# Result tiles of an output projection that start as loads and take products straight from PSUM

## The chip, the cores and the metric

The kernel runs on one core of a Trainium2 chip. The metric is the device time of one execution in microseconds (us); lower is better. The engines are TensorE (PE; PEld is its weight load), VectorE (DVE), ScalarE (ACT), GpSimd (POOL) and SyncE (SP), which issues most DMAs.

## The reference

One layer of a hybrid encoder on two sequences, a sample of 1024 tokens and a prompt of 512, with D_MODEL 2048, in float32:

```
h = rms_norm(x, norm_g)
z = h @ w_in                                  # c_val, c_glu, c_gate, q, k, v, a_gate
conv_out = conformer_conv(...) * silu(c_gate) # depthwise 31 taps, layer norm, silu, @ w_pw
attn_out = banded_sink_attention(q, k, v) * silu(a_gate)
x = x + concat([conv_out, attn_out]) @ w_out
y = rms_norm(x, final_norm_g)
```

The change is in the sample's `@ w_out`, `+ x` and the sum of squares for its final norm.

## The kernel before

**Products.** Each float32 operand is split into a high and a low part (`parts`: ACT copies the high part, DVE subtracts for the low one), and a product is three matmul passes. Big projections are done by `Unit`: a pair of output column tiles, eight 128-row slices of the contraction and two halves of 512 tokens form a 2x2 by 2x2 block product, made with seven block products of 12 matmuls (128x512) each instead of eight. They run in the order `ALONE`: P1, P2, P6, P5, P7, P3, P4. P1, P6, P7 and P4 add up in one PSUM bank (tag `a`, two buffers), P5 and P3 in another (`c`), P2 is alone in the third (`b`). After a product its bank is read (`tap`, written into the program after the first three matmuls of the next product, with a raised priority). The next product of the same bank, mostly two products later, may only start when the tap has read it.

**Taps before.** `Unit.tap` (L223) takes a result tile with `E()`, which alternates between the pools `g` and `u` of four 128x512 buffers each, and ACT copies the bank into it for P1, P6, P5, P7 and P4. P2 and P3 are added into a tile by DVE (L243), and P7's tile gets P5's by another DVE add. A finished tile goes to `finish`: with a first half of the contraction it is stored to `part`; with the second (`total`) a POOL DMA adds `part` into it (`add_into`, L435), and the tile is put on `later` with a count `landing` of 5, which `turn_over` counts down once per product.

**The sample's output projection.** `Mix.units` makes eight pairs of column tiles. `over[0]` is the first eight units (the contraction's second half, the attention part, stored as partial sums), `over[1]` the second eight (`total`). The first two units of `over[1]` run interleaved on more banks (`side`). `project` then loads the matching tile of x into a `p` tile (L1269), adds it (L1272), stores `y_d`, squares on ACT (L1279) and adds the squares into `sv` (L1281). `Mix.finish` later reads `y_d` back and scales it, beside the prompt's last stage.

**What runs around it.** Before `over[0]` come the pointwise convolutions of the two halves of the sample (L589 matmuls), after `over[1]` the prompt's pointwise convolution (`fj`, L589 again, with gates loaded into `g` tiles, L1484, and used by DVE at L1489) and its projection (`last_run`, L1714). Other work is cut into steps that lanes hand out per matmul: `conv` (depthwise convolution of the prompt, L920), `attn` (the prompt's attention, L1073 to L1115) and `prep`. A lane's `rate` is how much of its work is put into the program per time of matmuls. After `attention_sums` the attention lane's rate is `LATE`, 0.9; what is left is drained before the last unit of `over[0]`. `conv_sums` (inside `over[0]`) loads two 128x1024 `f` tiles four times and forms four sums of their halves in four `E()` tiles (`block_sums`, L1188 to L1191). `switch` loads and splits the token operands of `over[1]` during the last unit of `over[0]`, into `p` and `a` tiles (L797); attention's probabilities use `p` tiles too.

**Order.** Each engine executes its instructions in the order that a scheduler gave them when the program was built; SP likewise issues its DMAs in a fixed order, and a DMA whose buffer is not free holds up those behind it.

Of the kernel before, what the change touches and what calls it, by code (L numbers as in the profile page):

```python
# [10 lines left out]
ALU = mybir.AluOpType  # L11
# [22 lines left out]
W = 512  # L34
SOON = 800
PM = 18
LATE = 0.9
RUSH = 1.8
LANDING = 4
LOAD = 4500  # L40
# [11 lines left out]
BANK = {"P1": 0, "P2": 1, "P6": 0, "P5": 2, "P7": 0, "P3": 2, "P4": 0}  # L52
# [38 lines left out]
class Unit:  # L91
# [34 lines left out]
    late = False  # L126
# [50 lines left out]
    def open(self):  # L177
        e = self.e
        tags = ("s", "s", "pt") if self.side else ("a", "b", "c")
        self.bank = [None] * 3  # L180
        self.tags = tags

    def product(self, step, late):
        e, nc = self.e, self.e.nc
        name = self.order[step]
        p, o = OPERAND[name]
        i = self.at[p]
        e.w_prep(i + 1)
        hl = e.hl[i]
        n = BANK[name]  # L190
        if name in FRESH:
            self.bank[n] = e.PS(self.tags[n], [W])
        acc = self.bank[n]
        toks = e.T[SUMS[name]]
        for j in range(HALF):
            for q, (l, r) in enumerate(((0, 0), (0, 1), (1, 0))):
                nc.tensor.matmul(  # L197
                    acc,
                    hl[:, l, o, j, :],
                    toks[j][:, r],  # L200
                    start=name in FRESH and j == 0 and q == 0,
                    stop=name in LAST and j == HALF - 1 and q == 2,
                    skip_group_check=True,
                )
# [12 lines left out]
    def tap(self, name):  # L217

        e, nc = self.e, self.e.nc
        bank = self.bank[BANK[name]]  # L220
        if name not in ("P2", "P3"):
            t = e.E()
            nc.scalar.activation(t, bank, AF.Copy)  # L223
        if name == "P1":
            self.d[0, 0] = t
        elif name == "P6":
            self.d[0, 1] = t
        elif name == "P5":
            self.p5 = t
        elif name == "P2":  # L230
            self.add((0, 0), bank)
        elif name == "P7":
            self.d[1, 1] = t
            self.add((1, 1), self.p5)
            self.p5 = None
# [10 lines left out]
    def finish(self, n):  # L246
        e = self.e
        part, d = self.part[n[0]][n[1]], self.d.pop(n)
        if self.total:

            e.add_into(d, part)
            e.later.append([self.landing, self.done(n[0], n[1], d)])
        else:
            e.store(part, d)


class Plain(Unit):
# [407 lines left out]
class Sequence:  # L665
# [502 lines left out]
class Mix:  # L1168
# [26 lines left out]
    def attention_sums(self):  # L1195

        e, nc, seq = self.e, self.e.nc, self.seq
        for j in range(HALF):
# [13 lines left out]
            yield 4000  # L1212
        e.attn.rate = LATE

    def conv_sums(self):
        e, nc = self.e, self.e.nc
        for j in range(HALF):
            x = [e.F([TS]) for _ in range(2)]
            for t, k in zip(x, (j, j + HALF)):
                nc.sync.dma_start(t, self.xT[k])  # L1220
            yield 2 * LOAD
            self.block_sums(0, j, *x)
            yield 4000

    def fill(self):

        e = self.e
        e.T = {}
        held = deque()

        def load(step):
            if step < 7:
                held.append(self.load_sum(SUMS[ALONE[step]], 1, True, e.F))

        def put(step):
            for j, x in enumerate(held.popleft()):
                self.token_sum(SUMS[ALONE[step]], 1, j, x)

        load(0)
        load(1)  # L1240
        for step in range(4):
            yield 2 * LOAD
            put(step)
            load(step + 2)
        self.put, self.load = put, load

    def units(self):
        e = self.e
        out = []
        for o in range(0, ND, 2):  # L1250
            part = [[e.tc.dram_tile([P, W], F32, name=f"part_out{o}_{t}{c}") for c in range(2)] for t in range(2)]
            done = lambda t, c, z, o=o: self.project(o + c, t, z)

            def one(g, last, o=o, part=part, done=done):
                u = Unit(e, e.a["w_out"], (o, o + 1), 2 * HALF * g, part, done if last else None)
                c, n = divmod(o // 2, W // P)
                u.sums = {p: d[c][:, HALF * g : HALF * g + HALF, n * P : n * P + P] for p, d in self.wsum_d.items()}
                u.late = True
                u.landing = LANDING + 1
                return u  # L1260

            out.append(one)
        return out

    def project(self, o, t, z):
        e, nc = self.e, self.e.nc
        cols = slice(t * W, t * W + W)
        x = e.PT("p", NP, [W])
        nc.sync.dma_start(x, self.seq.xT[o][:, cols])  # L1269

        def steps():
            nc.vector.tensor_tensor(z, z, x, ALU.add)  # L1272
            e.store(self.y_d[o][:, cols], z)
            yield
            if not self.summed:
                self.sv = e.F([2, W])
            s = self.sv[:, t]
            if t in self.summed:
                nc.scalar.activation(x, z, AF.Square)  # L1279
                yield  # L1280
                nc.vector.tensor_tensor(s, s, x, ALU.add)  # L1281
            else:
                nc.scalar.activation(s, z, AF.Square)
            self.summed.add(t)
            yield

        return steps()

    def finish(self):
        e, nc = self.e, self.e.nc  # L1290
# [445 lines left out]
def encoder(ctx, tc, a):  # L1736
    e = Encoder(ctx, tc, a)
# [3 lines left out]
    last = LastPost(e, prompt, 0, a["y_p"], mix.wsum_d)  # L1741
# [172 lines left out]
    for n, half in enumerate(halves):  # L1914
        fj = half.first_jobs()
# [12 lines left out]
    over = [[u(1, False) for u in out], [u(0, True) for u in out]]  # L1928
# [17 lines left out]
    over[1][-1].before.append(e.prep.drain)  # L1946
    for step in range(2):
        over[1][-1].after[step] = [lambda i=i: last.split(i) for i in range(4 * step, 4 * step + 4)]
    jobs += grouped(over[0], None) + grouped(over[1], e.A)

    fj = last.first_jobs()
    over[1][-1].after[2] = [lambda: e.prep.add(last.attention_parts())]
# [60 lines left out]
```

## Time and profile before

| | |
|---|---|
| median of 3 runs | 2138.85 us (2136.21 to 2144.22) |
| the profiled execution | 2134.43 us, its span 2132.6 us, mean granted PE clock 0.992 |
| PE busy | 2073.8 us, 97% of the span |
| DVE busy | 1733.4 us, 81% |
| ACT busy | 1084.6 us, 51% |
| POOL busy | 105.0 us, 5% |

In the profile, a row of instructions has the line, the engine, the operation and `out<-in` with the buffer numbers left out; in square brackets or behind the last bar stands the idle time of the engine before it and what ended that. Matmul records overlap, so a group of 12 that takes 2.72 us in the chain of waits shows some 2.9 us in the timeline. On the time axis the sample's output projection lies from 1547 to about 1870 us: `over[0]` to about 1700, then `over[1]`. The prompt's pointwise convolution follows to about 1954, then the prompt's projection to 2120.

### The profile page before, as it was taken

The page shows a single profiled execution, that of the slowest core. Times are in us where ns is not written, and L with a number is a line of the kernel's source. Part 1 is how long each engine was busy: PE and PEld are TensorE (multiplying, and loading weights), DVE is VectorE, ACT ScalarE, POOL GpSimd, SP SyncE. Part 2 cuts the span into 40 slices and gives each one's busy share as a digit, 9 for nine tenths or more (in the row PEclk, how much of TensorE's full clock was granted, in tenths as well). Part 3 has the DMA queues.
Part 4 walks back from the last instruction along what each step waited for, and adds up shares of the span by engine and source line. Part 5 has one row for each costly group of instructions (what it writes and reads, how often), then busy time and mean ns, then how long its engine had stood idle before and what let it go on. Part 6 is the DMA issues. An engine that isn't in the chain of part 4 may idle for free.

```text
span 2132.6 us, 27077 instructions
## 1 busy us (share of the span) xinstructions
PE 2073.8 (97%) x9234; PEld 1697.0 (80%) x9234; DVE 1733.4 (81%) x2823; ACT 1084.6 (51%) x1762; POOL 105.0 (5%) x124
## 2 busy tenths in 40 slices
PE   8999999999999999999999999999999989998997
PEld 7878888888887888788888888878877867786875
DVE  8757899998899999998477787578888577978866
ACT  6475435333453444544456765344644464554444
POOL 0001110000011111000000000000000001110000
PEclk9999999999999999999999999999999999998999
DMA  8888887855676777755465647986886579997898
GB/s 287 305 290 243 200 222 233 288 191 176 210 225 168 182 181 183 247 168 168 126 225 155 195 140 268 329 286 209 285 279 224 163 248 298 249 306 244 288 300 290
DMA packets 269914, 494.54 MB, mean 232 GB/s; under 512 B 23632, under 2 KB 107984, under 8 KB 269776
## 3 DMA queue, kind: packets, MB, share of 16 engines
q1 hardware_dynamic: 252496, 461.35, 65.5%
q0 software_dynamic: 17280, 31.46, 9.1%
q8 instruction: 72, 1.18, 0.2%
q14 instruction: 66, 0.54, 0.1%
HBM read 331.77 MB, written 160.96 MB: 231 GB/s over the span
## 4 chain that ended last, share of the span: by engine, by line
PE 74%; DMA 11%; DVE 9%; issue 2%; ACT 2%; SPq 1%; ACTq 0%; POOL 0%; DVEq 0%; POOLq 0%
PE a L197 22%; PE a L589 12%; PE c L197 11%; PE c L589 6%; PE b L589 6%; PE b L197 5%; PE s L197 2%; PE pv L1102 2%; DVE hl L445 2%; PE s L1073 2%; PE pt L1107 1%; DMA f<-x_s 1%; DMA raw<-w_out 1%; PE a L1714 1%; DMA a<-ag_d 1%
## 5 line engine op out<-in xcount | busy, mean ns | idle before, releaser
L197 PE MATMUL a<-t,hl 128*128 128x512 f32 x2640 | 637.1, 392 | 18.7 <-ACT u L223 7.6
L197 PEld LDWEIGHTS a<-t,hl 128*128 128x128 f32 x2640 | 495.5, 189 | 129.4 <-ACT u L223 11.9
L444 ACT ACTIVATE hl<-raw 128x1024 fp32r<-128x1024 f32 (+1 forms) x356 | 323.8, 910 | 398.9 <-DVE raw L139 87.2
L445 DVE TENSOR_TENSOR hl<-raw,hl 128x1024 fp32r<-128x1024 f32 (+1 forms) x356 | 369.4, 1038 | 170.5 <-ACT hl L444 162.9
L589 PE MATMUL a<-t,hl 128*128 128x512 f32 x1344 | 330.5, 396 | 5.6 <-DVE f L1489 5.1
L197 PE MATMUL c<-t,hl 128*128 128x512 f32 x1320 | 320.4, 390 | 2.9 <-ACT g L223 1.9
L589 PEld LDWEIGHTS a<-t,hl 128*128 128x128 f32 x1344 | 250.7, 190 | 57.5 <-ACT t L444 5.5
L197 PEld LDWEIGHTS c<-t,hl 128*128 128x128 f32 x1320 | 247.2, 188 | 55.8 <-ACT g L223 3.0
L957 DVE SCALAR_TENSOR_TENSOR f<-f,c_w_dw,f 128x512 f32<-128x512 f32 x248 | 175.3, 748 | 0.3
L589 PE MATMUL c<-t,hl 128*128 128x512 f32 x672 | 165.0, 394 | 0.0
L920 DVE SCALAR_TENSOR_TENSOR f<-f,c_w_dw,f 128x512 f32<-128x512 f32 x232 | 163.2, 746 | 0.9 <-ACT f L915 0.9
L589 PE MATMUL b<-t,hl 128*128 128x512 f32 x672 | 163.4, 392 | 0.3 <-DVE hl L445 0.3
L197 PE MATMUL b<-t,hl 128*128 128x512 f32 x660 | 161.0, 390 | 0.0
L589 PEld LDWEIGHTS b<-t,hl 128*128 128x128 f32 x672 | 125.0, 188 | 25.5 <-DVE hl L445 0.7
L589 PEld LDWEIGHTS c<-t,hl 128*128 128x128 f32 x672 | 124.8, 188 | 24.5
L197 PEld LDWEIGHTS b<-t,hl 128*128 128x128 f32 x660 | 123.5, 188 | 25.2
L223 ACT ACTIVATE u<-a 128x512 f32<-128x512 f32 x115 | 68.1, 594 | 85.9 <-PE a L197 75.7
L223 ACT ACTIVATE g<-a 128x512 f32<-128x512 f32 x105 | 62.2, 593 | 77.9 <-PE a L197 74.9
L949 DVE SCALAR_TENSOR_TENSOR f<-f,w_both,f 128x512 f32<-128x512 f32 x120 | 89.8, 748 | 1.8
L352 ACT ACTIVATE hl<-raw 128x1024 fp32r<-128x1024 f32 x44 | 46.4, 1056 | 60.0 <-PE a L589 22.3
L445 DVE TENSOR_TENSOR a<-pt,a 128x512 fp32r<-128x512 f32 x64 | 44.0, 687 | 39.5 <-ACT a L444 38.8
L1087 ACT ACTIVATE p<-p,tiny 128x384 f32<-128x384 f32 (+1 forms) x96 | 54.5, 569 | 27.2 <-DVE tiny L1084 15.3
(337 smaller groups left out, 2583.8 us busy)
## 6 DMA issues: line engine op xcount, KB each, us to landing
raw<-w_in SPq DMA_DIRECT2D x171, 512.0 KB, 5.1
raw<-wsum_P SPq DMA_DIRECT2D x32, 512.0 KB, 4.8
raw<-w_out SPq DMA_DIRECT2D x31, 512.0 KB, 4.9
raw<-w_pw SPq DMA_DIRECT2D x24, 512.0 KB, 5.0
raw<-w_out SPq DMA_DIRECT2D x48, 256.0 KB, 4.9
wsum_P<-raw SPq DMA_DIRECT2D x47, 256.0 KB, 4.1
p<-xT_s SPq DMA_DIRECT2D x40, 256.0 KB, 5.6
f<-x_s SPq DMA_DIRECT2D x16, 512.0 KB, 7.0
```

The costliest lines, as they stand in the source:

```text
L197: nc.tensor.matmul(acc, hl[:, l, o, j, :], toks[j][:, r], start=name in FRESH and j == 0 and q == 0, stop=name in LAST and j == HALF - 1 a ...
L223: nc.scalar.activation(t, bank, AF.Copy)
L352: e.nc.scalar.activation(t[:, 0], raw, AF.Copy)
L444: nc.scalar.activation(hi, x, AF.Copy)
L445: nc.vector.tensor_tensor(lo, x, hi.bitcast(F32), ALU.subtract)
L589: nc.tensor.matmul(job.acc[0], hl[:, l, kk // HALF, kk % HALF, :], r, start=i == 0 and p == 0, stop=i == nk - 1 and p == 2,)
L920: nc.vector.scalar_tensor_tensor(t, h[:, j : j + T], w(j), t, ALU.mult, ALU.add)
L949: nc.vector.scalar_tensor_tensor(m0, odd[:, j : j + H], both(j), m0, ALU.mult, ALU.add)
L957: nc.vector.scalar_tensor_tensor(out, d[:, j : j + H], w(2 * j + k), out if j else m0, ALU.mult, ALU.add)
L1073: nc.tensor.matmul(ps[:, 0:n], qs[:, x, h], k[y][:, keys], start=p == 0, stop=p == 2)
L1087: nc.scalar.activation(p[:, 0:n], p[:, 0:n], AF.Exp, bias=nm[:, h : h + 1], accum_out=l[:, h : h + 1])
L1102: nc.tensor.matmul(pv, v[x][:, vs], pt[:, y], start=i == 0 and p == 0, stop=i == last and p == 2)
```

## The change

- A new class `Onto` replaces `Unit` for the sample's output projection. A result tile is taken with `E()` and filled by a DMA before its first product: with the tile of x (`over[0]`) or with the partial sums (`over[1]`). Each tap is one DVE add of the bank into the tile, for all seven products. A finished tile is stored at once; the POOL adding DMA, the tile of x in `project` and its add are gone. ACT reads no bank here.
- A tile's load is put into the program one product ahead of the product that it first takes (`ahead`), the first tile of a unit in the last product of the unit before (`next`); the interleaved pair has `ahead` 0, and the first tile of all is loaded before the last job of the stage before.
- `project` stores `y_d` directly and puts only the squares on `later`, with a count of 1.
- `conv_sums` forms its four sums in place in the two `f` tiles (`sums_in_place`) and takes no `E()` tiles.
- `LATE` is 1.2 instead of 0.9.

```diff
-LATE = 0.9
+LATE = 1.2
...
+class Onto(Unit):
+    late = True
+    START = {"P1": (0, 0), "P6": (0, 1), "P5": (1, 1), "P4": (1, 0)}
+    REST = {"P2": (0, 0), "P7": (1, 1), "P3": (0, 1)}
...
+    def begin(self, n):
+        if n not in self.d:
+            self.d[n] = self.e.E()
+            self.e.nc.sync.dma_start(self.d[n], self.source(*n))
...
+    def product(self, step, late):
+        step_of = step + self.ahead
+        if step_of < len(self.order):
+            name = self.order[step_of]
+            if name in self.START:
+                self.begin(self.START[name])
+        elif self.next:
+            self.next.begin((0, 0))
+        return super().product(step, late)
+
+    def tap(self, name):
+        n = self.START.get(name) or self.REST[name]
+        d = self.d[n]
+        self.e.nc.vector.tensor_tensor(d, self.bank[BANK[name]], d, ALU.add)
+        if name in self.REST or name == "P4":
+            del self.d[n]
+            if self.total:
+                self.done(n[0], n[1], d)
+            else:
+                self.e.store(self.part[n[0]][n[1]], d)
...
-            self.block_sums(0, j, *x)
+            self.sums_in_place(0, j, *x)
...
+        nc.vector.tensor_tensor(d, b, d, ALU.add)
+        nc.vector.tensor_tensor(b, a, b, ALU.subtract)
+        nc.vector.tensor_tensor(a, d, a, ALU.subtract)
+        nc.vector.tensor_tensor(c, c, a, ALU.subtract)
...
-                u = Unit(e, e.a["w_out"], (o, o + 1), 2 * HALF * g, part, done if last else None)
+                if last:
+                    u = Onto(e, e.a["w_out"], (o, o + 1), 2 * HALF * g, lambda t, c: part[t][c], None,
+                             lambda t, c, z: self.project(o + c, t, z))
+                else:
+                    x = lambda t, c: self.seq.xT[o + c][:, t * W : t * W + W]
+                    u = Onto(e, e.a["w_out"], (o, o + 1), 2 * HALF * g, x, part)
...
-                u.late = True
-                u.landing = LANDING + 1
...
     def project(self, o, t, z):
-        x = e.PT("p", NP, [W])
-        nc.sync.dma_start(x, self.seq.xT[o][:, cols])
+        e.store(self.y_d[o][:, t * W : t * W + W], z)
 
         def steps():
-            nc.vector.tensor_tensor(z, z, x, ALU.add)
-            e.store(self.y_d[o][:, cols], z)
-            yield
...
             if t in self.summed:
+                x = e.PT("p", NP, [W])
                 nc.scalar.activation(x, z, AF.Square)
...
-        return steps()
+        e.later.append([1, steps()])
...
+    chain = over[0] + over[1]
+    for u, v in zip(chain, chain[1:]):
+        u.next = v
...
+    for u in over[1][:2]:
+        u.ahead = 0
+    over[1][0].next = None
+    fj[-1].before.append(lambda: chain[0].begin((0, 0)))
```

More of the change, by code (lines that the diff above doesn't have):

```diff
@@ L254, in finish, with __init__, open @@
             e.store(part, d)
+class Onto(Unit):
+    late = True
+    START = {"P1": (0, 0), "P6": (0, 1), "P5": (1, 1), "P4": (1, 0)}
+    REST = {"P2": (0, 0), "P7": (1, 1), "P3": (0, 1)}
+    def __init__(self, e, w, cols, k, source, part, done=None):
+        super().__init__(e, w, cols, k, part, done)
+        self.source, self.next, self.ahead = source, None, 1
+    def begin(self, n):
+        if n not in self.d:
+            self.d[n] = self.e.E()
+            self.e.nc.sync.dma_start(self.d[n], self.source(*n))
+    def open(self):
+        super().open()
+        self.begin((0, 0))
+    def product(self, step, late):
[17 more added lines that the diff above has]
+                self.e.store(self.part[n[0]][n[1]], d)
 class Plain(Unit):
@@ L1221, in conv_sums, with sums_in_place @@
             yield 2 * LOAD
-            self.block_sums(0, j, *x)
+            self.sums_in_place(0, j, *x)
             yield 4000
+    def sums_in_place(self, g, j, x0, x1):
+        e, nc = self.e, self.e.nc
+        a, b, c, d = x0[:, :W], x0[:, W:], x1[:, :W], x1[:, W:]
+        nc.vector.tensor_tensor(d, b, d, ALU.add)
+        nc.vector.tensor_tensor(b, a, b, ALU.subtract)
+        nc.vector.tensor_tensor(a, d, a, ALU.subtract)
+        nc.vector.tensor_tensor(c, c, a, ALU.subtract)
+        for name, t in (("S1", d), ("S3", b), ("S2", a), ("S4", c)):
+            e.store(self.sums_d[g, name][j], t)
     def fill(self):
@@ L1251, in units, with one @@
             part = [[e.tc.dram_tile([P, W], F32, name=f"part_out{o}_{t}{c}") for c in range(2)] for t in range(2)]
-            done = lambda t, c, z, o=o: self.project(o + c, t, z)
-            def one(g, last, o=o, part=part, done=done):
-                u = Unit(e, e.a["w_out"], (o, o + 1), 2 * HALF * g, part, done if last else None)
+            def one(g, last, o=o, part=part):
+                if last:
[4 more added lines that the diff above has]
+                    u = Onto(e, e.a["w_out"], (o, o + 1), 2 * HALF * g, x, part)
                 c, n = divmod(o // 2, W // P)
                 u.sums = {p: d[c][:, HALF * g : HALF * g + HALF, n * P : n * P + P] for p, d in self.wsum_d.items()}
-                u.late = True
-                u.landing = LANDING + 1
                 return u
@@ L1266, in project @@
         e, nc = self.e, self.e.nc
-        cols = slice(t * W, t * W + W)
-        x = e.PT("p", NP, [W])
-        nc.sync.dma_start(x, self.seq.xT[o][:, cols])
+        e.store(self.y_d[o][:, t * W : t * W + W], z)
         def steps():
-            nc.vector.tensor_tensor(z, z, x, ALU.add)
-            e.store(self.y_d[o][:, cols], z)
-            yield
             if not self.summed:
```

## The prediction

> **What bounds the kernel now.** I read the page's first part, then the windows by stage, then PE's own timeline for its idle gaps.
>
> ```profile
> span 2132.6 us, 27077 instructions
> PE 2073.8 (97%) x9234; PEld 1697.0 (80%) x9234; DVE 1733.4 (81%) x2823; ACT 1084.6 (51%) x1762; POOL 105.0 (5%) x124
> ```
> ```profile
> core 0: us, PE busy (x) PEld busy (x) DVE busy (x) ACT busy (x) POOL busy (x), PEclk, DMA share, GB/s
> 1546.00:1641.00 95.00, 91.43 (x414) 74.71 (x414) 85.42 (x146) 41.29 (x72) 0.00 (x0) 1.00 0.79 265
> 1546.00:1700.00 154.00, 150.43 (x684) 123.88 (x684) 117.94 (x204) 71.58 (x131) 0.00 (x0) 1.00 0.69 226
> 1700.00:1870.00 170.00, 158.16 (x680) 126.44 (x679) 130.79 (x208) 96.13 (x164) 20.94 (x24) 0.97 0.90 261
> 1870.00:1956.00 86.00, 77.86 (x331) 63.69 (x330) 71.21 (x101) 44.64 (x71) 6.95 (x8) 0.95 0.95 297
> 1813.00:1832.00 19.00, 19.00 (x85) 15.74 (x84) 18.90 (x28) 11.50 (x20) 3.48 (x4) 1.00 0.84 220
> ```
>
> PE bounds the kernel. The changed program has the same 9214 matmuls as the old one (counted in the two built programs), so only PE's gaps and its lowered clock can be won. PE is idle 3.6 us in `over[0]` (second window), 11.8 us in `over[1]` (third), 8.1 us in the prompt's convolution behind it (fourth). These are the gaps over half a microsecond:
>
> ```profile
> 1592.35 3.03 PE L197 MATMUL a<-t,hl 128*128 128x512 f32 x12 [2.09 <-ACT u L223]
> 1603.91 0.73 PE L197 MATMUL a<-t,hl 128*128 128x512 f32 x2 [1.15 <-ACT hl L444]
> 1723.39 8.59 PE L197 MATMUL a<-t,hl 128*128 128x512 f32 x36 [2.00 <-ACT u L223]
> 1746.20 5.78 PE L197 MATMUL a<-t,hl 128*128 128x512 f32 x12 [3.18 <-ACT hl L444]
> 1788.64 3.03 PE L197 MATMUL c<-t,hl 128*128 128x512 f32 x12 [0.99 <-ACT u L223]
> 1803.05 4.60 PE L197 MATMUL a<-t,hl 128*128 128x512 f32 x12 [3.22 <-ACT g L223]
> 1851.21 0.50 PE L197 MATMUL c<-t,hl 128*128 128x512 f32 x1 [0.74 <-ACT g L223]
> 1866.74 3.01 PE L197 MATMUL a<-t,hl 128*128 128x512 f32 x12 [1.18 <-ACT u L223]
> 1931.93 7.97 PE L589 MATMUL a<-t,hl 128*128 128x512 f32 x24 [5.06 <-DVE f L1489]
> 1953.86 1.62 PE L1714 MATMUL a<-hl,t 128*128 128x512 f32 x3 [3.08 <-DVE f L1489]
> ```
>
> Six of the ten wait for the old tap's ACT copy. ACT is not slow there (96 of 170 us busy): the copy waits for a tile. The chain of waits and the timeline show it for the 3.22 us gap:
>
> ```profile
> 1763.17 2.72 PE c L197 x12
> 1782.77 6.00 DMA p<-xT_s
> 1794.32 4.11 DMA y_d<-g
> 1802.52 0.49 ACT g L223
> ```
> ```profile
> 1787.99 0.60 ACT L223 ACTIVATE u<-c 128x512 f32<-128x512 f32 x1 [4.62 <-DMA y_d<-u]
> 1788.86 0.69 DVE L1272 TENSOR_TENSOR u<-u,p 128x512 f32<-128x512 f32 x1 [6.11 <-DMA p<-xT_s]
> 1795.30 0.89 POOL L435 DMA_DIRECT2D g<-part_out x1 [13.75 <-DMA y_d<-u]
> ```
>
> A finished tile is held through the adding DMA, five counts of `landing`, x's load and its add, and the store; until that ends its buffer serves no tap. A stall costs twice: after gaps of 0.99 and 2.09 us twelve matmuls take 3.03 us, after 3.18 and 3.22 us they take 5.78 and 4.60.
>
> **The change part by part.** Sums are made against the profiled execution, 2134.43 us; the median of the runs lies 4.4 us higher, and I move it by the same difference.
>
> *Tile waits.* With the change a tap takes no buffer. A finished tile is stored at once, and the next load of its buffer is issued far ahead: following semaphores and queue orders in the built program, I counted the matmuls between the last one that a tile's load depends on and the first one that needs it. For 62 of the 64 loads it is 61 or more, so 13.8 us at 2.72/12 = 0.227 us each. What has to fit, by the rows below: the store (5.9), the load (5.6), the add (0.69), 12.2 us in all. I take all five waits in the two stages outside `switch`, 2.09+0.99+3.22+0.74+1.18 = 8.2 us, and the slow matmuls after one, 4.60-3.03 = 1.6: **-9.8** (bounds 0 and -9.8).
>
> ```profile
> p<-xT_s SPq DMA_DIRECT2D x40, 256.0 KB, 5.6
> u<-part_out POOLq DMA_DIRECT2D x17, 256.0 KB, 7.1
> y_d<-u SPq DMA_DIRECT2D x17, 256.0 KB, 5.9
> ```
>
> *Switch.* The 2.00 and 3.18 us gaps, and 5.78-3.03 = 2.75 after, are those of the last unit of `over[0]`, where what is left of attention is drained and `over[1]`'s operands come in through the same `p` tiles. There the chain runs
>
> ```profile
> 1739.40 5.48 DMA a<-msum_S
> 1744.90 0.63 ACT t L444
> ```
>
> At the rate 1.2 attention's last matmul is the 7447th instead of the 7633rd, before that unit starts at the 7574th, and the operand loads' distances grow: the tightest was 14 matmuls (3.2 us, less than a landing), now 49 (11.1 us). Of 7.9 us I take **-6** (bounds 0 and -7.9), since the late ACT copy has other inputs.
>
> *Gates.* The 5.06 and 3.08 us gaps and 7.97-24x8.59/36 = 2.2 us of slow matmuls wait for L1489, whose gates land late:
>
> ```profile
> 1934.53 5.47 DMA g<-gate_d
> 1947.71 5.29 DMA g<-gate_d
> ```
>
> Their `g` tiles and SP's queue were held by the last units' x loads, adds and stores. Counted as above, the distances of these loads grow by 24 matmuls or more for six of eight, 5.4 us each. That covers both gaps: of 10.4 us, **-8** (bounds 0 and -10.4), the rest for other loads ahead of them on SP.
>
> *What is added.* Per unit ACT loses five copies, and DVE has seven adds from PSUM. In `over[0]` it had three, so four more per unit; in `over[1]` it had three and four adds of x, so none more. A DVE add from PSUM costs what one from SBUF does:
>
> ```profile
> L243 DVE TENSOR_TENSOR u<-c,u 128x512 f32<-128x512 f32 x29 | 19.9, 685 | 3.6 <-PE c L197 2.8 <-ACT u L223 0.8
> L243 DVE TENSOR_TENSOR g<-b,g 128x512 f32<-128x512 f32 x27 | 18.5, 686 | 4.8 <-PE b L197 4.8
> L1272 DVE TENSOR_TENSOR u<-u,p 128x512 f32<-128x512 f32 x17 | 11.4, 686 | 8.1 <-DMA p<-xT_s 6.9 <-DMA u<-part_out 1.2
> L223 ACT ACTIVATE u<-a 128x512 f32<-128x512 f32 x115 | 68.1, 594 | 85.9 <-PE a L197 75.7
> ```
>
> But four taps of a unit (P1, P6, P5, P7) must end within the one product that lies between, 2.72 us, and they now stand in DVE's queue behind weight splits and convolution taps. In `over[0]` DVE's 117.9 us become 117.9+32x0.69 = 140 of 154. In its first five units 85.4+20x0.69 = 99.2 us meet 95 us: DVE is over-full by 4.2 us there, and I charge PE **+4** (bounds 0, if the reserve of 2.72-0.69 = 2.0 us per tap absorbs it, and +14, all of the added work). The cover is that reserve; gone, each late tap stalls PE by what it is late. In `over[1]` I charge nothing for DVE: in the window 1813 to 1832 it was busy 18.90 of 19.00 us and PE lost nothing, and L243 g<-b shows DVE waiting for PE, not the reverse.
>
> *Two late loads.* P5's tiles of the fourth and sixth unit of `over[1]` stand in SP's queue behind weight loads: distances of only 39 and 43 matmuls, 8.8 and 9.7 us, for a tap, a split, four issues, a landing of 5.6 and an add, some 9 us. DVE would sit in that wait, and behind it stand weight splits needed a product later. **+2** for both (bounds 0 and +4).
>
> *Hidden.* 32 loads move from POOL's adding DMA and 32 of x from `over[1]` to `over[0]`; SP issues 32 more there at DMA share 0.69, and `over[1]` (0.90) gets lighter. The sums in place are four DVE operations as before. The 1.15 us gap stays. I charge 0.
>
> Sum: -9.8-6-8+4+2 = -17.8, so 2134.43 becomes 2116.6, and the median 2138.85 becomes **2121 us**.
>
> **The skill against it.** After 3.18 us of idle time the trace shows 2.75 us more for the next twelve matmuls, after 2.09 us none. The Trainium skill, "TensorE: Matmul & The Clock Gate", "HAM oscillation — how this bites in real kernels", warns only of idle gaps over about 3.4 us; by that the slow matmuls after the 3.18 and 3.22 us gaps would be no saving, and the sum 4.3 us smaller. The rows decide. And the Trainium skill, "TensorEngine Tiling (Array Packing)", "PSUM Bottleneck", advises reading PSUM out with ScalarE and VectorE both, which the change gives up; that speaks for the first rival here.
>
> **The rivals.**
>
> *DVE becomes the bound (slower).* Outside the interleaved pair 14x4 = 56 taps have a deadline of one product. If DVE runs late, each stalls PE, and the convolution and attention steps in its fixed order cannot give way. It takes the whole gain of 23.8 us at a mean of 23.8/56 = 0.43 us beyond the reserve; at 0.7 us it costs 39 us: 2138.85-23.8+39 = **2154**. For it: 99 us of work in 95. Against it: the full window at 1813, and that L243's adds waited for PE.
>
> *Only the tile waits go (about the same).* ACT's and DMA's lateness at `switch` and at the gates has other roots (DMA shares 0.90 and 0.95), so 9.8 us go, and DVE's 4 come: 2138.85-5.8 = **2133**.
>
> *The loads are no better than the copies.* A tap then waits for a load where the old one waited for a tile: only the five waits' shape changes, 2139. The distances speak against it; I count it with the second rival.
>
> **How the numbers follow.** Forecast case 0.62, the second rival 0.24, DVE as the bound 0.14. A measurement of this kernel can tell about 0.5%, 10.7 us, from no change: below 2128.2 is faster. The forecast case by its bounds runs from 2138.85-28.1 = 2111, less the 4.4 us by which the profiled execution lay lower, 2106, to about 2130; a small part of it falls within 0.5%, and a small part of the second rival below. Faster 0.65, same 0.22, slower 0.13. For eight in ten the range takes in the second rival to no change and a little above: 2106 to 2142; left out is most of the DVE case.
>
> **What would show it.** Right: no gap over 1 us before an L197 matmul that waits for a tap, except near P3 of the fourth and sixth unit of `over[1]`; `over[0]`'s DVE near 140 us; L1489's waits for gates under 2 us together; the prompt's projection starting some 18 us earlier. Wrong: many gaps of 0.3 to 1.5 us released by the DVE add in `over[0]`'s first five units (DVE case), or the gaps at `switch` and L1489 as before (second rival).

## The result and the profile after

The changed kernel takes **2108.11 us** (median of 4 runs, 2107.31 to 2110.99) against 2138.64 us for the kernel before on the same chip: ratio **0.9856**, 95% interval 0.9835 to 0.9877, 30.5 us faster. Its profiled execution takes 2107.31 us, 27.1 us less than the one of before; its mean granted PE clock is 0.997 instead of 0.992.

The page's first lines, and the windows that the prediction showed of before (us of the stretch, then busy us of PE, PEld, DVE, ACT and POOL, the granted clock, DMA share and GB/s):

```profile
span 2105.5 us, 26965 instructions
PE 2063.2 (98%) x9234; PEld 1689.4 (80%) x9234; DVE 1751.4 (83%) x2855; ACT 1043.0 (50%) x1682; POOL 77.1 (4%) x92
```
```profile
1546.00:1700.00 154.00, 151.34 (x693) 123.53 (x692) 137.87 (x245) 58.36 (x114) 0.00 (x0) 1.00 0.86 279
1700.00:1870.00 170.00, 167.81 (x739) 137.35 (x738) 149.62 (x230) 82.60 (x125) 0.00 (x0) 1.00 0.80 262
```

PE's idle time in the second window falls from 11.8 to 2.2 us. Over the whole of `over[0]` and `over[1]` DVE has 22.5 us more to do than before, about the 32 adds of 0.69 us that the prediction counted. The windows of that stage, of before and of after:

```profile
1546.96:1899.52 352.56, 337.14 (x1490) 273.96 (x1489) 273.93 (x448) 188.05 (x326) 26.72 (x31) 0.99 0.82 248
```
```profile
1552.78:1885.78 333.00, 328.16 (x1463) 268.14 (x1462) 296.45 (x481) 148.11 (x249) 0.00 (x0) 1.00 0.83 272
```

These are PE's gaps of half a microsecond and more from PE's timeline of the changed kernel, 1590 to 1990 us (new line numbers: the tap is L290, the parts are L486 and L487):

```profile
1638.42 0.96 PE L197 MATMUL c<-t,hl 128*128 128x512 f32 x3 [1.25 <-DVE u L290]
1640.15 0.74 PE L1144 MATMUL pv<-a,f 128*128 128x512 f32 x2 [0.55 <-DVE a L487]
1800.31 3.04 PE L197 MATMUL c<-t,hl 128*128 128x512 f32 x12 [0.61 <-DVE u L290]
1813.35 2.97 PE L197 MATMUL a<-t,hl 128*128 128x512 f32 x12 [0.94 <-DVE u L290]
1842.99 3.06 PE L197 MATMUL c<-t,hl 128*128 128x512 f32 x12 [0.52 <-DVE u L290]
```

None of the ten gaps of before is left, and no matmul runs at a lowered clock behind the new ones. Where the time went, by the first matmul of each stage in PE's timelines (`over` is `over[0]` and `over[1]`):

| us | starts before | after | length before | after | difference |
|---|---|---|---|---|---|
| all up to `over` | 0 | 0 | 1547.0 | 1552.8 | +5.8 |
| `over` | 1546.96 | 1552.78 | 352.6 | 333.0 | -19.6 |
| prompt's convolution (L589, now L631) | 1899.52 | 1885.78 | 54.3 | 43.5 | -10.8 |
| prompt's projection (L1714, now L1764) to the end | 1953.86 | 1929.30 | 178.7 | 176.2 | -2.5 |

The first row grows in part because attention's higher rate puts 27 attention matmuls ahead of `over` that stood in it before (1490 PE instructions in the windows above before, 1463 after). a_late09 below, which has the old rate, starts `over` at 1551.79 too, so how much of the 5.8 us they explain is open. The first two rows belong together, -13.7 us. By PE's timeline of before `over[1]` ends at 1899.52 us, not at about 1870 as the introduction to the profile has it; none of the gaps lies between.

### The profile page after: what moved, and what is told of

Same layout as the page of the kernel before. It is cut to its first block, busy times and chain, and to the rows that moved or that the text cites. A ratio compares the mean times of both kernels' runs of the same rounds, so it can differ in the third digit from the quotient of the medians.

```text
span 2105.5 us, 26965 instructions
## 1 busy us (share of the span) xinstructions
PE 2063.2 (98%) x9234; PEld 1689.4 (80%) x9234; DVE 1751.4 (83%) x2855; ACT 1043.0 (50%) x1682; POOL 77.1 (4%) x92
## 5 line engine op out<-in xcount | busy, mean ns | idle before, releaser
L486 ACT ACTIVATE hl<-raw 128x1024 fp32r<-128x1024 f32 (+1 forms) x356 | 323.9, 910 | 433.6 <-DVE raw L139 93.9
L487 DVE TENSOR_TENSOR hl<-raw,hl 128x1024 fp32r<-128x1024 f32 (+1 forms) x356 | 369.2, 1038 | 153.5 <-ACT hl L486 152.8
L631 PE MATMUL a<-t,hl 128*128 128x512 f32 x1344 | 328.1, 394 | 0.5 <-DVE hl L487 0.5
L631 PEld LDWEIGHTS a<-t,hl 128*128 128x128 f32 x1344 | 248.2, 188 | 50.9 <-DVE hl L487 1.0
L999 DVE SCALAR_TENSOR_TENSOR f<-f,c_w_dw,f 128x512 f32<-128x512 f32 x248 | 175.2, 746 | 0.3
L631 PE MATMUL c<-t,hl 128*128 128x512 f32 x672 | 165.5, 394 | 0.0
L631 PE MATMUL b<-t,hl 128*128 128x512 f32 x672 | 163.4, 392 | 0.2 <-DVE hl L487 0.2
L631 PEld LDWEIGHTS b<-t,hl 128*128 128x128 f32 x672 | 125.0, 188 | 25.3 <-DVE hl L487 0.6
L631 PEld LDWEIGHTS c<-t,hl 128*128 128x128 f32 x672 | 125.1, 189 | 24.4
L223 ACT ACTIVATE u<-a 128x512 f32<-128x512 f32 x82 | 48.6, 592 | 57.4 <-PE a L197 55.3
L223 ACT ACTIVATE g<-a 128x512 f32<-128x512 f32 x78 | 46.2, 593 | 56.1 <-PE a L197 54.1
L486 ACT ACTIVATE a<-pt 128x512 fp32r<-128x512 f32 x64 | 37.9, 592 | 67.9 <-PE pt L1149 67.6
```

What stands on the lines that cost most here:

```text
L486: nc.scalar.activation(hi, x, AF.Copy)
L487: nc.vector.tensor_tensor(lo, x, hi.bitcast(F32), ALU.subtract)
L631: nc.tensor.matmul(job.acc[0], hl[:, l, kk // HALF, kk % HALF, :], r, start=i == 0 and p == 0, stop=i == nk - 1 and p == 2,)
L999: nc.vector.scalar_tensor_tensor(out, d[:, j : j + H], w(2 * j + k), out if j else m0, ALU.mult, ALU.add)
```

## The experiments

Medians, their ratios to runs of the kernel before on the same chip, and the same stages in each profiled execution:

| kernel | median us | ratio to before | up to `over` | `over` | convolution | projection to the end |
|---|---|---|---|---|---|---|
| before | 2138.85 | | 1547.0 | 352.6 | 54.3 | 178.7 |
| after | 2108.11 | 0.9856 (0.9835 to 0.9877) | 1552.8 | 333.0 | 43.5 | 176.2 |
| b_late12 | 2131.53 | 0.9968 (0.9956 to 0.9980) | 1554.8 | 342.0 | 56.5 | 180.6 |
| a_late09 | 2144.30 | 1.0032 (1.0019 to 1.0045) | 1551.8 | 370.2 | 43.5 | 175.4 |
| h0_first_half | 2118.66 | 0.9915 (0.9889 to 0.9941) | 1553.0 | 328.0 | 51.9 | 181.0 |
| h1_second_half | 2136.15 | 0.9992 (0.9974 to 1.0011) | 1550.3 | 353.3 | 47.8 | 177.6 |
| a_hold5 | 2111.96 | 0.9885 (0.9869 to 0.9902) | 1554.7 | 332.7 | 44.5 | 178.2 |
| b_no_x | 2137.48 | 0.9991 (0.9975 to 1.0007) | 1549.3 | 357.9 | 51.4 | 178.7 |
| b_late12_no_x | 2121.42 | 0.9915 (0.9902 to 0.9929) | 1556.3 | 331.9 | 50.0 | 179.7 |
| a_esums | 2124.80 | 0.9946 (0.9931 to 0.9960) | 1552.7 | 348.9 | 43.5 | 177.3 |
| a_dve256 | 2135.07 | 0.9991 (0.9978 to 1.0003) | 1556.9 | 354.8 | 43.5 | 179.6 |
| h0_gate_early | 2114.62 | 0.9888 (0.9874 to 0.9901) | 1556.2 | 328.5 | 43.5 | 184.1 |
| imp2_gate | 2103.87 | 0.9833 (0.9816 to 0.9849) | 1556.3 | 327.1 | 43.5 | 175.2 |
| ig_late15 | 2109.19 | 0.9857 (0.9836 to 0.9878) | 1559.1 | 324.7 | 43.5 | 177.7 |

### The rate alone, and all but the rate

The kernel before with `LATE` 1.2, and the changed kernel with 0.9:

```diff
-LATE = 0.9
+LATE = 1.2
```

> The kernel before with attention's rate 1.2 and nothing else. Theory (each part of the gain belongs to tiles that are held too long, and each place has its own cause): only the switch's 7.9 us go (the 2.00 and 3.18 us gaps and the slow matmuls after), since the tightest operand load there has 49 matmuls instead of 14; the gaps in over[1] (0.99, 3.22, 0.74, 1.18) and the gates' waits at L1489 stay. 2138.6 - 8 = about 2131. Rival (the rate alone explains the result: attention out of the way relieves everything behind it): 2115 or less, with the gaps of over[1] and the gates gone too.

2131.53 us, as the theory had it. Of the switch's gaps 0.30 us is left; those of `over[1]` are there as before. The 1.15 us gap of `over[0]`, on which the expectation says nothing, is gone too: apart from the 2.62 us below, no gap there is over 0.42 us. The profiled execution is the slowest of the ten (2135.63 us), so its stages in the table do not show the median's gain. PE's timeline:

```profile
1592.96 5.53 PE L197 MATMUL a<-t,hl 128*128 128x512 f32 x16 [2.62 <-ACT u L223]
1729.69 5.78 PE L197 MATMUL a<-t,hl 128*128 128x512 f32 x24 [0.30 <-ACT u L223]
1788.24 5.74 PE L197 MATMUL a<-t,hl 128*128 128x512 f32 x24 [1.09 <-ACT g L223]
1800.65 4.45 PE L197 MATMUL a<-t,hl 128*128 128x512 f32 x12 [3.95 <-ACT g L223]
```

> The changed kernel with attention's rate back at 0.9. Theory: the switch's 7.9 us come back, since its operand loads again have 7 to 46 matmuls (1.6 to 10.4 us) where a landing takes 5.6; besides, attention's sums now take tiles beside the loads of x, four of which have only 13 to 37 matmuls (3 to 8 us): some 5 to 11 us more. over[1]'s later part and the gates stay as in the changed kernel. 2108 + 13 to 19 = 2121 to 2127. Rival (the rate alone explains the result): 2135 or more, with waits for the gates. Rival (taps alone explain it): 2108 to 2112.

2144.30 us, 36.2 us above the changed kernel and 17 us beyond the theory's worst case. The time is in the range of the rival that the rate alone explains the result, but the waits for the gates that it names are not there (the convolution takes 43.5 us), and b_late12 rules it out. The rate is worth 7.6 us on the old taps and about 36 us on the new ones: the two edits don't add up, and the new taps without the rate gain nothing. Two gaps show why. First PE's timeline, then the chain of waits ahead of its first line (start, length, what):

```profile
1615.17 4.70 PE L197 MATMUL a<-t,hl 128*128 128x512 f32 x12 [10.76 <-DVE u L290]
1782.15 4.83 PE L197 MATMUL a<-t,hl 128*128 128x512 f32 x12 [9.30 <-DVE u L290]
```
```profile
1603.12 5.45 DMA msum_S<-f
1608.59 0.32 SPq L1262
1608.96 5.37 DMA u<-xT_s
1614.42 0.70 DVE u L290
```

A load of x stands in SP's queue behind a load of `conv_sums` (L1262), which waits for its `f` tile until the sums' store has ended. So x's load starts at 1608.96, and PE waits for a store, a landing and an add, one after the other. The second gap is the switch: its chain has `DMA p<-mix_d` from 1772.80 for 7.31 us, the ACT copy and the DVE split behind it, and the tap behind that in DVE's order. The expectation priced loads by the matmuls counted up to them, and so left out what a queued load of something else adds.

### One half alone

The new class in `over[0]` alone:

```diff
-                    u = Onto(... lambda t, c: part[t][c], None, ...)      # over[1]
+                    u = Unit(... part, lambda t, c, z: self.project(o + c, t, z))
+                    u.landing = LANDING + 1
...
-    chain = over[0] + over[1]
+    chain = over[0]
```

> The new class only in over[0] (tiles begin as x, sums in place, rate 1.2); over[1] has the old taps with ACT copies, the adding DMA and five counts of landing, but no load or add of x. Theory: over[1]'s four gaps (6.1 us and 1.6 us of slow matmuls) and the gates' waits (10.4 us; the gates' tightest loads have 49 and 57 matmuls again) stay, all else goes: 2108 + 18 = about 2126. Rival (the x loads and adds in over[1] were what held the tiles and the queue): about 2110, with the gates' waits gone.

2118.66 us, between the two, and neither was right as a whole. `over[1]`, with its old copies on ACT, adding DMA and five counts, has no gap above 0.3 us, as the rival had it; the last gate's wait stays, as the theory had it, with one for a copy on ACT ahead of it:

```profile
1909.87 5.69 PE L631 MATMUL a<-t,hl 128*128 128x512 f32 x24 [1.47 <-ACT t L486]
1932.92 1.62 PE L1766 MATMUL a<-hl,t 128*128 128x512 f32 x3 [6.20 <-DVE f L1541]
```

Its `over` is even 5.0 us shorter than the changed kernel's. What it loses it loses behind that, 8.4 and 4.8 us.

The other half alone, with x loaded and added in `project` as before:

```diff
-                    u = Onto(e, e.a["w_out"], (o, o + 1), 2 * HALF * g, x, part)      # over[0]
+                    u = Unit(e, e.a["w_out"], (o, o + 1), 2 * HALF * g, part)
```

> The new class only in over[1] (tiles begin as the partial sums); over[0] has the old taps, and project loads and adds x as before; sums in place and rate 1.2 stay. Theory: a finished tile is still held for x's load and add, so five loads of partial sums have only 14 to 43 matmuls (3 to 10 us) against the 9 or so they need, 8 us of stalls in all; the first 2.09 and 1.15 us gaps of over[0] stay, and the gates' waits stay in part (tightest loads 49 and 58): 2108 + 8 + 3 + 5 to 10 = 2124 to 2129. Rival (the adding DMA on POOL with its 7.1 us landing was what held the tiles): about 2112.

2136.15 us: no gain, 7 us more than the theory gave it. PE's timeline shows these gaps before taps:

```profile
1743.76 5.14 PE L197 MATMUL a<-t,hl 128*128 128x512 f32 x12 [4.49 <-DVE g L290]
1791.80 4.60 PE L197 MATMUL c<-t,hl 128*128 128x512 f32 x12 [2.28 <-DVE u L290]
1862.38 5.49 PE L197 MATMUL c<-t,hl 128*128 128x512 f32 x12 [2.61 <-DVE u L290]
```

By the chain of waits, the first is a load of partial sums (1738.10, 4.89 us) that stands in SP's queue behind loads of x, which wait for a tile that a DVE split frees. The second is such a load behind a store of weight sums (1784.87, 6.15 us), the third is DVE's other work. The gaps of 2.09 and 1.15 us in `over[0]` were to stay and are gone, though its taps are the old ones; the largest left there is 0.87 us. So the adding DMA was not what the gain came from: without it, but with x's loads and adds, nothing is won.

### What held the tiles: a longer hold, and x left out

```diff
         if name in self.REST or name == "P4":
             del self.d[n]
-            if self.total:
-                self.done(n[0], n[1], d)
-            else:
-                self.e.store(self.part[n[0]][n[1]], d)
+            self.e.later.append([5, self.let(n, d)])      # let does these four lines
```

> The changed kernel with one thing added: a finished tile is not stored at once but after five more products, as long as the old kernel counted for its adding DMA. No engine and no transfer has more to do. Theory (a tile's lifetime sets when loads into it can start): the gates' tightest loads have 49, 57 and 57 matmuls again instead of 73, 81, 81, so their waits come back, 6 to 10 us as in the kernel before and with the new class in over[0] alone; one load of partial sums (near the end of over[1]) has 17 matmuls, 3.9 us, for some 8 to 9 it needs: 4 to 5 us. 2108 + 10 to 15 = 2118 to 2123. Rival (the gates wait for other transfers, for x's loads and adds or for the adding DMA on the queues, not for tiles): 2108 to 2112.

2111.96 us, 3.9 us slower by medians with intervals that overlap, and in the rival's range. The gates, though counted 49 and 57 matmuls ahead as in h0_first_half, cost 1.1 us instead of 6.2:

```profile
1931.79 0.93 PE L1768 MATMUL a<-hl,t 128*128 128x512 f32 x3 [0.77 <-DVE f L1543]
1934.16 11.84 PE L1768 MATMUL a<-hl,t 128*128 128x512 f32 x44 [0.33 <-DVE f L1543]
```

A hold of five products is nearly free, as long as nothing else keeps the tile. Then x's load and add alone, left out of the old kernel, at both rates:

```diff
-        x = e.PT("p", NP, [W])
-        nc.sync.dma_start(x, self.seq.xT[o][:, cols])
...
-            nc.vector.tensor_tensor(z, z, x, ALU.add)
```

> The kernel before, at its rate of 0.9, with x neither loaded nor added in project (this leaves x out of the sample's result); the taps with ACT's copies, the adding DMA and the five counts of landing stay. Theory as forecast (the copy waits for a tile that is held through adding DMA, counts, x and store): part of over[1]'s gaps goes, the rest stays, 2133 to 2136. Second theory, after the run with the new class in over[0] alone (there over[1] had no gap although its adding DMA and counts had stayed): x's load and add were the whole of it, so 7 to 9 us of gaps in over[1] go, the switch's and the gates' stay: 2130. If the gates' waits go too: 2120.

2137.48 us: no difference. The switch takes 6.33 us, there is one gap of 4.53 us in `over[1]`, and the last gate is 5.42 us late:

```profile
1755.53 4.70 PE L197 MATMUL a<-t,hl 128*128 128x512 f32 x12 [6.33 <-ACT hl L444]
1812.46 5.20 PE L197 MATMUL a<-t,hl 128*128 128x512 f32 x12 [4.53 <-ACT g L223]
1958.54 1.62 PE L1712 MATMUL a<-hl,t 128*128 128x512 f32 x3 [5.42 <-DVE f L1487]
```

> The kernel before with rate 1.2 and without x's load and add in project (x is left out of the sample's result). It has over[1] exactly as in the run with the new class in over[0] alone, behind the old over[0]. Theory (the old over[1] lost PE time only through x's loads and adds; the same edit showed nothing at rate 0.9 because the switch got worse by as much): over[1]'s gaps of 1.09, 3.95, 0.74, 1.12 us and 1.4 us of slow matmuls go, the first gap of over[0] and the gates' waits stay: 2131.5 - 8 = 2123. Rival (the old taps lose time in over[1] whatever they wait for, and it was over[0]'s relief that carried over): 2129 to 2133, with gaps of 3 us or more in over[1].

2121.42 us, 10.1 us below b_late12 (8 were expected): with the switch out of the way, `over[1]` has no gap above 0.3 us, while the first gap of `over[0]` and the gate's stay (2.61 and 5.61 us). So at the rate 1.2 x's load and add were what cost `over[1]` its gaps, and the copies, the adding DMA and the counts were not. At the rate 0.9 leaving x out wins nothing: the switch takes 3.15 us more than before, and ahead of the 4.53 us gap DVE waits for a weight load instead of x's. DVE's timeline, b_no_x and then b_late12_no_x at the same instruction:

```profile
1804.21 0.69 DVE L139 TENSOR_TENSOR raw<-raw,raw 128x512 f32<-128x512 f32 x1 [6.38 <-DMA raw<-w_out]
```
```profile
1787.36 0.69 DVE L139 TENSOR_TENSOR raw<-raw,raw 128x512 f32<-128x512 f32 x1 [1.55 <-DMA raw<-w_out]
```

The load of x was not parted from its add.

### The sums in place

```diff
-            self.sums_in_place(0, j, *x)
+            self.block_sums(0, j, *x)
```

> The changed kernel with the convolution's four sums in four result tiles again instead of in place. Theory: the sums take result tiles whose next use is a load of x; eight of these loads then have only 19 to 56 matmuls (4.3 to 12.7 us; 19, 19, 31, 35, 40, 40, 41, 54) where 7 to 9 us are needed: 4 + 4 + 2 + 1 = about 11 us more, 2119 (2112 to 2125), all of it in over[0]. Rival (the sums in place are a detail): 2108.

2124.80 us, 16.7 us slower: the upper end of what was expected, and nearly all of it in `over` (348.9 against 333.0 us). The largest gap, by PE's timeline, and the load it waits for, by the chain:

```profile
1594.77 0.79 PE L197 MATMUL a<-t,hl 128*128 128x512 f32 x1 [7.19 <-DVE u L290]
```
```profile
1588.73 5.27 DMA u<-xT_s
```

### DVE's reserve

```diff
+        self.e.nc.vector.tensor_tensor(d[:, :256], d[:, :256], d[:, :256], ALU.max)
         self.e.nc.vector.tensor_tensor(d, self.bank[BANK[name]], d, ALU.add)
```

> The changed kernel with a useless DVE operation of half a tile (128x256, about 0.34 us busy, 0.3 us of the queue) ahead of each of the 112 taps of the sample's output projection, which leaves the result as it is. It adds 34 us to DVE: 155 of 154 us in over[0], 166 of 170 in over[1] by the windows of the changed kernel. Theory (a tap has a reserve of about 2 us, and only DVE's total can be overrun): 3 to 10 us, 2111 to 2118. Rival (a later tap stalls PE each time, the mechanism of the slower case of the prediction): 56 to 112 taps by 0.3 us, 17 to 34 us, 2125 to 2142.

2135.07 us, 27.0 us slower: inside the rival's bounds. These are the two groups of the added operation and the window of `over`:

```profile
L290 DVE TENSOR_TENSOR u<-u 128x256 f32<-128x256 f32 x62 | 25.3, 415 | 3.3 <-DMA u<-xT_s 2.8 <-DMA u<-part_out 0.4
L290 DVE TENSOR_TENSOR g<-g 128x256 f32<-128x256 f32 x49 | 20.3, 417 | 9.1 <-DMA g<-part_out 5.5 <-DMA g<-xT_s 3.5
1556.85:1911.68 354.83, 335.76 (x1463) 270.84 (x1462) 331.13 (x591) 147.29 (x249) 0.00 (x0) 0.98 0.78 254
```

DVE is busy 331 of 355 us there, 296 of 333 us in the changed kernel. The two groups' records add up to 45.6 us, but DVE's records overlap, and its busy time in the window grows by 34.7 us, as expected. By its total alone DVE would still fit into the old length, 331 of 333 us; `over` is 21.8 us longer, 0.2 us for each of 112 taps. So it is not only DVE's total that counts. It does not come tap by tap either: 4.70 us stand in one gap, where the switch's splits fill DVE's order, and 4.02 in another, at 1870 us. So the changed kernel has DVE time for its own 22 us of added taps and not for another 35; from which amount on PE loses was not tried.

### Two ways to go further

The gates one job earlier, on h0_first_half:

```diff
     fj = last.first_jobs()
+    gates = [job.before[0] for job in fj]
+    for n, job in enumerate(fj):
+        job.before = gates[n + 1 : n + 2] if n else gates[:2]
```

> The new class in over[0] alone, as before, and each gate of the prompt's convolution loaded one job (24 matmuls, 5.4 us) earlier; nothing else changes. Theory: the gates' waits (1.5 and 6.2 us, and the slow matmuls after) came from gate loads that stood in SP's queue behind weight loads that wait for DVE's splits, so they go: 2118.7 - 8 to 11 = 2108 to 2111, over[1] without a gap as it was. If the last stage keeps the changed kernel's length besides, 2104 to 2106. Rival (the prompt's convolution is held by DVE's other work, and the gates are only the last to come): 2116 to 2119.

2114.62 us: 4.0 us gained by medians where the theory had 8 to 11, with intervals that overlap and profiled executions 1.55 us apart. The convolution itself has no wait any more (43.5 us), but the last gate is still late by 4.62 us, now just behind the projection's first matmuls. In the chain the gate's load stands in SP's queue behind a load of the prompt's x (L1649), which waits for a tile that a DVE split (L487) frees:

```profile
1923.87 0.61 DVE t L487
1924.49 0.34 SPq L1649
1925.55 5.58 DMA g<-gate_d
```

So the rival holds in part, though the time lies below its range: behind the gates stands DVE's order.

The changed kernel with the same edit, and its own remaining waits taken away:

```diff
-            yield 2 * LOAD
+            yield 3 * LOAD
             self.sums_in_place(0, j, *x)
...
+    over[1][3].ahead = over[1][5].ahead = 2
```

> The changed kernel with the convolution's four sums called later after their loads (three times 4500 ns of matmuls instead of twice), the two late tiles of partial sums loaded two products ahead instead of one, and the gates a job earlier. Theory: the stalls at 1638 (1.25 and 0.55 us) and at the two late loads (0.61, 0.52) go, 3 us: 2105. Rival (these waits are taken up by others, DVE's order above all): 2108.

2103.87 us, the fastest: `over` is 5.9 us shorter, of which the time ahead of it takes 3.5 us back in the profiled execution, and one gap above half a microsecond is left in it, 1.16 us at 1742. By medians it is 4.2 us below the changed kernel, measured on another chip; the two intervals (0.9816 to 0.9849, 0.9835 to 0.9877) overlap, so that gain is likely, not certain. Its three edits were not parted.

> The last version (sums called later, two tiles loaded two products ahead, gates a job earlier) with attention's rate 1.5 instead of 1.2. Theory (the rate is worth what the operand loads at the switch gain, and these are no longer the tightest at 1.2): counted in the built program the switch's loads keep their 49 to 61 matmuls, while four loads of x in over[0] fall to 40 to 54 (9 to 12 us, where a store, a landing and an add took 12.2 us with the store and 6.3 without): 0 to 4 us slower, 2104 to 2108. Rival (attention further ahead relieves over[0]'s end once more, as from 0.9 to 1.2): 2096 to 2100.

2109.19 us: a rate of 1.5 brings nothing more, and the loss of 5 us is 1 us more than expected (the intervals overlap here too). By the profiled executions `over` ends at the same time in both (1883.7 and 1883.4 us), and 2.5 us are lost in the projection, not at the loads of x. So the rate's gain ends by 1.2; that it ends because the switch's loads have time enough by then is argued, not shown.

## Why the prediction was right, and where not

The forecast, 2121 us, lay 12.9 us too high; the result is in the range, near its lower end. By profiled executions -17.8 us were forecast and -27.1 came.

- **Tile waits, -9.8:** the amount was right; all five gaps went, with the slow matmuls. The mechanism, "the copy waits for a tile", is not what the traces show for the two largest. In the chain that the prediction shows for the 3.22 us gap the store has landed at 1798.43, 4 us ahead of the copy. Between them stands work in DVE's and ACT's fixed orders: DVE had waited 6.11 us for x's load, so its weight work came late, ACT's splits behind that, and the tap's copy directly behind those. The 2.09 us gap, in `over[0]`, has no x in it: DVE waited for a load of `conv_sums`. ACT's timeline of before for the first of the two, then DVE's and ACT's for the second:

```profile
1800.94 1.06 ACT L444 ACTIVATE hl<-raw 128x1024 fp32r<-128x1024 f32 x1 [2.49 <-DVE raw L139]
1802.42 0.58 ACT L223 ACTIVATE g<-a 128x512 f32<-128x512 f32 x1
```
```profile
1587.38 0.69 DVE L1188 TENSOR_TENSOR g<-f,f 128x512 f32<-128x512 f32 x1 [2.44 <-DMA f<-mix_d]
1591.18 0.63 ACT L444 ACTIVATE hl<-g 128x512 fp32r<-128x512 f32 x1 [2.92 <-DVE g L139]
1591.72 0.58 ACT L223 ACTIVATE u<-a 128x512 f32<-128x512 f32 x1
```

  This fits the runs: a longer hold alone costs little (a_hold5), another late load in x's place gives the same kind of gap (b_no_x), and without x at the rate 1.2 the gaps of `over[1]` are gone (h0_first_half, b_late12_no_x). It is read from the traces; no run delays a load of DVE's alone. That -9.8 came out is in part luck.
- **Switch, -6 of 7.9:** b_late12 shows that the rate did it, -7.6 us by medians, as argued; the discount "since the late ACT copy has other inputs" was not needed.
- **The 1.15 us gap that "stays"** went as well, and by the rate: it is there in b_no_x at 0.9 (1.15 us at 1609.96) and gone in b_late12.
- **Gates, -8 of 10.4:** all of it went (-10.8 us in the stage), but the reason given failed. Distances counted in matmuls do not order these waits: a_hold5 and h0_first_half have the same ones (49, 57, 57), and in both SP issued the last gate loads at the same time. These are their lines of SP's timeline, h0_first_half and then a_hold5:

```profile
1925.76 0.92 SPq L1613 DMA_DIRECT2D raw<-w_out  x2
1926.73 2.11 SPq L1536 DMA_DIRECT2D g<-gate_d  x3
```
```profile
1925.75 0.92 SPq L1615 DMA_DIRECT2D raw<-w_out  x2
1926.72 1.45 SPq L1538 DMA_DIRECT2D g<-gate_d  x3
```

  The gate stands behind a weight load that waits for DVE's split, and is issued when that chain allows it. In h0_first_half PE came to the convolution at 1881.04 us, in a_hold5 at 1887.34: the one waits 6.2 us for the last gate, the other 1.1. Time won in `over[1]` is given back there unless that chain is earlier too. In the changed kernel it is, by its line of SP's timeline, and why it is 5 us earlier there was not settled:

```profile
1921.63 1.45 SPq L1534 DMA_DIRECT2D g<-gate_d  x3
```
- **DVE, +4, and the late loads, +2:** all gaps left in `over` come to 4.4 us. The late loads were found where they were forecast, at 1800 and 1843, and cost 1.1 us; their landings took 6.20 and 6.03 us by the chain of waits.

  DVE's total held, 137.87 us against the forecast of 140. What it cost was of another kind than an over-full first five units: 0.94 us at 1813 behind other work, and 1.8 us at 1638, where DVE sat in a wait for `conv_sums`' load with a tap behind it. DVE's timeline:

```profile
1635.14 0.69 DVE L1270 TENSOR_TENSOR f<-f,f 128x512 f32<-128x512 f32 x1 [2.35 <-DMA f<-mix_d]
1637.68 0.68 DVE L290 TENSOR_TENSOR u<-c,u 128x512 f32<-128x512 f32 x1
```

- **The sums in place, 0:** right as a cost, but not as an edit without effect: undone, they cost 16.7 us. The 13.8 us that the prediction counted for most loads held only because of them.
- **Missing:** -2.5 us in the prompt's projection, which had no term.
- **The rivals:** "only the tile waits go" fell with the gates and the switch. DVE as the bound did not come true, but a_dve256 shows it no more than 35 us of added work away.

The mis-sized terms together: 1.9 for the switch, 1.2 for the gap, 2.8 for the convolution, 1.6 for the costs, 2.5 for the projection, 10.0 in all; 0.7 of it is lost again in small gaps that neither list has.

Of the signs that the prediction named, three came: `over[0]`'s DVE time near 140 us, no gap of PE that waits for the gates, and the prompt's projection earlier, by 24.6 us where it named 18. One did not quite: the gap of 1.25 us at 1638, before a matmul that waits for a tap, stands where none over 1 us was to be.

## What to carry to other kernels

A transfer on the way of a result tile costs by the queue it stands in: ask for each load what is issued ahead of it on its queue and what that waits for, and not only how many matmuls lie between. Then ask which engine sits in that wait, since what stands behind it in that engine's order comes late too: here mostly DVE, with weight splits and taps. Edits that relieve the same queue and the same tiles don't add up: here the rate was worth 7.6 us without the new class and 36 with it, and the sums in place 17 us with it (without it they were not tried), so an edit of a group is to be judged by undoing it in the finished kernel as well as by doing it alone. When PE becomes faster in one stage, look in the next for the load that will now be the last to come.

## What the hardware showed that was not expected

Whether the matmuls behind a PE gap run at a lowered clock is not a matter of the gap's length alone. These are windows of 5 us behind four gaps; the third figure from the end is the granted clock. First before, behind 2.46 us, and the changed kernel, behind 2.48 us, at the same place in the program:

```profile
889.36:894.36 5.00, 5.00 (x19) 4.33 (x20) 4.75 (x13) 2.41 (x10) 0.00 (x0) 0.71 0.55 152
```
```profile
891.73:896.73 5.00, 5.00 (x25) 4.29 (x26) 4.89 (x14) 2.77 (x11) 0.00 (x0) 1.00 0.67 176
```

Then h0_gate_early, behind 1.91 us, and a_dve256, behind 2.77 us:

```profile
2082.42:2087.42 5.00, 5.00 (x15) 3.97 (x16) 4.86 (x9) 2.82 (x5) 0.00 (x0) 0.66 0.80 263
```
```profile
1423.89:1428.89 5.00, 5.00 (x27) 4.25 (x28) 3.81 (x15) 1.52 (x2) 0.00 (x0) 1.00 0.49 173
```

The traces' clock records show an order in this. In each trace the stretches at 0.50 begin on one grid with steps of 3.41 us, and last one, two or three steps: 3.41, 6.83 or 10.24 us (the one that runs past the program's end aside). These are the step ahead of such a stretch in before, with the gap of 3.18 us, and the stretch of two steps:

```profile
1742.20:1745.60 3.40, 0.82 (x4) 0.36 (x2) 3.37 (x6) 3.08 (x6) 0.00 (x0) 1.00 1.07 333
1745.61:1752.43 6.82, 6.23 (x14) 4.57 (x15) 6.58 (x12) 4.16 (x7) 0.19 (x1) 0.50 1.07 333
```

The 14 traces have 48 such stretches between their first 10 and their last 60 us. In the step ahead, PE was idle for 1.71 us or more, half a step, in 47 of them (1.07 us in one). Of the other steps at full clock all but one (1.93 us) had at most 1.79 us of idle time. So the 1.91 us above, within one step, lowered the clock, and the 2.77 us, which fall across a step's end (1.22 and 1.55 us), did not. No run moved a gap along the grid on purpose. The prediction drew the line by length, between 2.09 and 3.18 us; the gap of 2.09 us in before also lies across a step's end, at 1592.01. The Trainium skill, "TensorE: Matmul & The Clock Gate", "HAM oscillation — how this bites in real kernels", draws it at about 3.4 us of idle gap; the traces here do not agree, since 1.91 us was enough.

And a DVE operation on 128x256 (the maximum of a_dve256) took 415 ns where an add of 128x512 took 685: if the time grows evenly with the length, about 145 ns of each do not depend on it (2x415-685).
